# Last feed-forward: two first-half products of six pairs made ahead, reciprocal roots on VectorE, prompt scores as full-height products

## The chip, the cores and the metric

One core of a Trainium2 chip. The metric is device time in microseconds (us) of one launch of the whole kernel, the median over runs. The core has four compute engines, each with its own queue of instructions: TensorE (PE in the profile, with PEld for its weight loads), VectorE (DVE), ScalarE (ACT) and GpSimd (POOL); SyncE (SP) issues the DMAs. Matmuls read SBUF and write PSUM.

## The reference

One step of a two-layer streaming encoder of width 1024 on 640 tokens: 512 of a new prompt and 8 x 16 of running streams. Layer 0 is a convolution module and a feed-forward; layer 1 attends to one shared K/V (16 heads of 64) and has the second feed-forward; a final norm ends it.

```python
def rms_norm(x, g):
    y = x * lax.rsqrt(jnp.mean(x * x, axis=-1, keepdims=True) + EPS)
    return y * g

def swiglu_ffn(h, g, w_in, w_out):
    a, b = jnp.split(rms_norm(h, g) @ w_in, 2, axis=-1)
    return h + (jax.nn.silu(a) * b) @ w_out
...
for l in range(2):
    h = conv_module(h, ...) if l == 0 else h + attention(h) @ w_o
    h = swiglu_ffn(h, norm_ffn[l], w_ffn_in[l], w_ffn_out[l])
return rms_norm(h, norm_final), ...
```

The hidden width of the feed-forward is 2816, that is 22 blocks of 128. Everything is float32.

## The kernel before, in words

Activations lie transposed: 1024 features as 8 tiles of 128 partitions, 640 tokens along the free axis (`h`). A float32 product is made from three products of a reduced type, fp32r: each operand is split into a high part (ScalarE copies it to fp32r) and a low part (VectorE subtracts the high part from the value), and TensorE forms high x high, high x low and low x high (`mm3`, L164 to L166). So each weight tile that comes in by DMA (`raw`) costs one ScalarE and one VectorE pass ahead of its matmuls: L144 and L148 in general, `hilo` (L904, L905) in the last feed-forward.

**Norms.** `colmean` squares the 8 feature tiles, adds `cut` of them up (L187, on GpSimd unless told otherwise) and forms the mean over partitions with tiny matmuls against a column of 1/1024 (L196). `rstd_bc` adds EPS (L217, VectorE), raises to the power -0.5 (L221, GpSimd) and `spread` copies the result to all partitions by a matmul (L208). Twelve places take such a root.

**Attention.** Pairs of heads, with the work of one pair beside the projections of the next. `head_a` makes one prompt head's scores: K lies in 64 of the 128 partitions. KK holds K's high part twice (both halves of the partitions), QQ holds Q's high part in one half and Q's low part in the other, so one product over 128 rows gives two of the three terms (L727); the third, Q high x K low, is a product over 64 rows (L728, KL from L715). The first block of 128 tokens is one plain float32 product over 64 rows (L725). The output projection (L873 adds it to `h`) is split by tokens into 384 and 256 (`SG`).

**The last feed-forward** (from `hf`). Its first matrix product is done as a 2 x 2 block product with seven block products in place of eight: the blocks are feature halves, token halves (320 each, `NH`) and, on the weights' side, the gate and the up columns of one block of 128 (a "pair", 22 of them). X11, X21, ... X22 name the seven operand tiles, kept as high and low parts (`XH`, `XL`), which are made once: `stats` and `xnorm` (L1002) normalise half 0, then half 1, `xsub` forms differences, `xput` (L1012, L1013) splits. `w_seven` makes the weights' side for each pair: four sums of 512 columns (L917 to L923, VectorE) and the splits, in five pieces, into a ring of three 2048-column tiles for each of high and low part; a pair uses two of them. `product` (L936) is one block product, 12 matmuls of 320 columns. `seven` runs the pair: X11, X21, XT2, XT1, XT3, XT4, X22, with ScalarE copies (`keep`, L945) and VectorE additions (`plus`, L951) between, then `gate` (L961) and the split of the hidden tile (L153, L154). The last two products of a pair come after the first ones of the next. After six pairs (four in the last chunk) the output product of that chunk follows (L1075 adds it).

**What sets the order.** A scheduler lists each engine's instructions once, at build time, by priorities (`tc.high_priority(offset=HP)` raises one); on the chip each engine runs its list in order, and waits where an operand is not ready. Tiles of a pool with `bufs=2` are taken in turn: the third user of a name waits for the first to be done.

Of the kernel before, what the change touches and what calls it, by code (L numbers as in the profile page):

```python
# [9 lines left out]
F32R = mybir.dt.float32r  # L10
AF = mybir.ActivationFunctionType
# [3 lines left out]
P = 128  # L15
# [28 lines left out]
HP = 2000  # L44
# [13 lines left out]
SG = ((0, 384), (384, 256))  # L58
# [15 lines left out]
def tile_trunk(ctx, tc, xT, vecs, hist, w_pw1, w_pw2, w_in0, w_out0, w_in1, w_out1,  # L74
# [38 lines left out]
    mhalf = cst.tile([P, 4], F32, name="mhalf", tag="mhalf")  # L113
    nc.gpsimd.memset(mhalf, -0.5)
# [61 lines left out]

    def colmean(st, pieces, n, cut, tag, eng=nc.gpsimd):
        nt = n // P
# [14 lines left out]
        for k, f in enumerate(srcs):  # L193
            s = f()
            for t in range(nt):
                nc.tensor.matmul(st[:, 512 + t * w + k:513 + t * w + k], s[:, t * P:(t + 1) * P],  # L196
                                 onec, start=True, stop=True)
# [8 lines left out]
    def spread(st, r, n):  # L206
        for t in range(n // P):
            nc.tensor.matmul(st[:, t * P:(t + 1) * P], r[:, t:t + 1].to_broadcast([P, P]), ident,  # L208
                             start=True, stop=True)
        return st[:, :n]  # L210

    def rstd_bc(pieces, n, engs=SQ, cut=CUT, r2=None, eng=nc.gpsimd):
        st = w2t()
        nt = n // P
# [6 lines left out]
        nc.gpsimd.tensor_tensor(out=r2[:, :nt], in0=r[:, :nt], in1=mhalf[:, :nt], op=ALU.pow)  # L221
# [478 lines left out]
    def head_a(p, hh):  # L700
# [14 lines left out]
        nc.vector.tensor_tensor(out=KL[r], in0=kt[r, P:], in1=KK[r].bitcast(F32), op=ALU.subtract)  # L715
# [3 lines left out]
        for i in ORD:  # L719
# [4 lines left out]
            if i == 0:  # L724
                nc.tensor.matmul(ps, qt[r, P:2 * P], kt[r, P:2 * P], start=True, stop=True)  # L725
            else:
                nc.tensor.matmul(ps, QQ[:, q], KK[:, 0:n], start=True, stop=False)  # L727
                nc.tensor.matmul(ps, QQ[r, q], KL[r, 0:n], start=False, stop=True)  # L728
# [137 lines left out]
    for g0, n in SG:  # L866
# [15 lines left out]

    mm = fpool("mm2", 6, space=PSUM)
    w2 = fpool("w2b", 1, space=PSUM)
    tp = fpool("tp1", 2)
    wx = fpool("wx", 1)
    xo = fpool("xo", 1)
    XH = xo.tile([P, 7, 4, NH], F32R, name="XH", tag="XH")
    XL = xo.tile([P, 7, 4, NH], F32R, name="XL", tag="XL")
    bcw = xo.tile([P, NT], F32, name="bcw", tag="bcw")  # L890
    xb = ExitStack()
    xt = xb.enter_context(tc.tile_pool(name="xt", bufs=1, reuse_waits="tile"))

    ring = [0]

    def wtile():
        ring[0] += 1
        pool, tag = (wx, "x") if ring[0] % 3 == 0 else (wp, "")
        return (pool.tile([P, 2048], F32R, tag=f"w{tag}hi", name=nm("whi")),
# [282 lines left out]
```

## Time and profile before

| | us |
|---|---|
| median of 3 runs | 1587.42 |
| lowest and highest | 1586.53 and 1593.77 |
| the profiled execution, its own time | 1588.73 |
| its span | 1586.9 |
| TensorE busy | 1500.3 |
| VectorE busy | 1042.2 |
| ScalarE busy | 670.0 |
| GpSimd busy | 401.0 |

The profiled execution had a mean TensorE clock of 0.979 of full speed. In the windows, each row is a stretch of the span (from:to, length), then for each engine busy us and instructions, then the granted clock, the DMA share and GB/s. In the timeline a row is start, duration, engine, line, operation, out<-in, partitions x columns; `64*128` ahead of the shape are the rows and columns of TensorE's array in use. Matmuls are pipelined: the start-to-start step, not the duration, is what one costs.

### The profile page before, as it was taken

What the parts mean: (1) busy time and instruction counts of PE and PEld (TensorE: products, weight loads), DVE (VectorE), ACT (ScalarE), POOL (GpSimd) and SP (SyncE); (2) the same over time, 40 slices, a digit from 0 to 9 for tenths busy, and PEclk for the clock granted to TensorE, in tenths of its full rate; (3) what the DMA queues carried; (4) which work ended last, traced back from release to release, by engine and by line L of the source; (5) the groups of instructions that cost most, each with busy time, mean ns of one, the idle gap of its engine ahead of it and who ended that gap; (6) DMA issues with size and microseconds to landing.
All of it is one profiled execution on the core that took longest, in us unless ns stands there. A gap on an engine that the chain in (4) does not pass through costs nothing.

```text
span 1586.9 us, 26564 instructions
## 1 busy us (share of the span) xinstructions
PE 1500.3 (95%) x10734; PEld 1412.2 (89%) x10734; DVE 1042.2 (66%) x1933; ACT 670.0 (42%) x1228; POOL 401.0 (25%) x368
## 2 busy tenths in 40 slices
PE   5988998999999999999999999998699999999997
PEld 5878898889999999999877887876599999999996
DVE  5895999978535545555665657554785565575565
ACT  4544454535423323234644444443453253253242
POOL 6954577867401000004221112111300000000001
PEclk9999999999999999999999999999799999999998
DMA  7784334444322343335445545451023123122211
GB/s 241 233 235 138 118 119 166 133 160 160 133 74 66 115 146 113 127 113 184 167 151 193 169 165 169 132 183 41 27 80 107 54 80 107 56 90 95 79 55 67
DMA packets 59659, 199.96 MB, mean 126 GB/s; under 512 B 10128, under 2 KB 22672, under 8 KB 46736
## 3 DMA queue, kind: packets, MB, share of 16 engines
q1 hardware_dynamic: 59248, 197.96, 37.7%
q8 instruction: 84, 1.38, 0.4%
q10 hardware_dynamic: 288, 0.31, 0.1%
q14 instruction: 39, 0.32, 0.1%
HBM read 187.02 MB, written 11.22 MB: 125 GB/s over the span
## 4 chain that ended last, share of the span: by engine, by line
PE 73%; DVE 15%; ACT 3%; DMA 3%; POOL 3%; issue 3%; SPq 0%; POOLq 0%; DVEq 0%; ACTq 0%
PE mm L936 17%; PE mm L164 16%; PE mm L166 16%; PE mm L165 16%; DVE w L428 5%; DVE wlo L148 4%; DMA raw<-in_w_pw 1%; PE w L783 1%; PE w L728 1%; DVE xl L154 1%; PE am L814 1%; PE am L768 1%; ACT whi L144 1%; DVE hid L154 1%; PE am L751 1%
## 5 line engine op out<-in xcount | busy, mean ns | idle before, releaser
L165 PE MATMUL mm<-xh,wlo 128*128 128x256 f32 (+1 forms) x1344 | 420.4, 314 | 13.0 <-DVE wlo L148 12.5
L164 PE MATMUL mm<-xh,whi 128*128 128x256 f32 (+1 forms) x1344 | 416.2, 314 | 5.7 <-ACT xh L153 3.6
L166 PE MATMUL mm<-xl,whi 128*128 128x256 f32 (+1 forms) x1344 | 416.6, 313 | 0.7 <-DVE xl L154 0.6
L165 PEld LDWEIGHTS mm<-xh,wlo 128*128 128x128 f32 x1344 | 259.5, 193 | 16.9 <-DVE wlo L148 15.2
L164 PEld LDWEIGHTS mm<-xh,whi 128*128 128x128 f32 x1344 | 257.3, 193 | 11.0 <-ACT xh L153 4.1
L166 PEld LDWEIGHTS mm<-xl,whi 128*128 128x128 f32 x1344 | 257.6, 192 | 2.5 <-DVE xl L154 2.1
L144 ACT ACTIVATE whi<-raw 128x2048 fp32r<-128x2048 f32 (+2 forms) x100 | 170.5, 1708 | 192.2 <-PE mm L166 138.3
L165 PE MATMUL mm<-hid,wlo 128*128 128x320 f32 (+2 forms) x704 | 215.7, 309 | 6.8 <-DVE wlo L148 6.8
L166 PE MATMUL mm<-hid,whi 128*128 128x320 f32 (+2 forms) x704 | 211.8, 308 | 0.2
L148 DVE TENSOR_TENSOR wlo<-raw,whi 128x2048 fp32r<-128x2048 f32 (+5 forms) x100 | 180.7, 1810 | 46.7 <-ACT whi L144 43.9
L164 PE MATMUL mm<-hid,whi 128*128 128x320 f32 (+2 forms) x704 | 210.9, 308 | 0.0
L936 PE MATMUL mm<-XH,whi 128*128 128x320 f32 x616 | 186.1, 314 | 6.2 <-ACT XH L1012 5.1
L936 PE MATMUL mm<-XH,wlo 128*128 128x320 f32 x616 | 191.0, 312 | 0.0
L936 PE MATMUL mm<-XL,whi 128*128 128x320 f32 x616 | 189.8, 311 | 0.0
L148 POOL TENSOR_TENSOR wlo<-raw,whi 128x1536 fp32r<-128x1536 f32 (+3 forms) x50 | 146.5, 2934 | 71.9 <-ACT whi L144 71.7
L165 PEld LDWEIGHTS mm<-hid,wlo 128*128 128x128 f32 x704 | 132.1, 188 | 8.0 <-DVE wlo L148 8.0
L166 PEld LDWEIGHTS mm<-hid,whi 128*128 128x128 f32 x704 | 131.4, 188 | 0.7 <-DVE hid L154 0.6
L164 PEld LDWEIGHTS mm<-hid,whi 128*128 128x128 f32 x704 | 130.7, 188 | 0.4
L221 POOL TENSOR_TENSOR rst<-rst,mhalf 128x2 f32<-128x2 f32 (+1 forms) x9 | 13.6, 1515 | 452.5 <-DVE rst L217 452.5
L936 PEld LDWEIGHTS mm<-XH,whi 128*128 128x128 f32 x616 | 115.6, 190 | 9.0 <-ACT XH L1012 5.8
L936 PEld LDWEIGHTS mm<-XH,wlo 128*128 128x128 f32 x616 | 117.4, 191 | 0.1
L936 PEld LDWEIGHTS mm<-XL,whi 128*128 128x128 f32 x616 | 116.8, 190 | 0.0
(188 smaller groups left out, 2485.3 us busy)
## 6 DMA issues: line engine op xcount, KB each, us to landing
raw<-in_w_in SPq DMA_DIRECT2D x62, 1024.0 KB
raw<-in_w_out SPq DMA_DIRECT2D x36, 768.0 KB
raw<-in_w_pw SPq DMA_DIRECT2D x22, 1024.0 KB
cache<-in_ck SPq DMA_DIRECT2D x32, 512.0 KB
cache<-in_cv SPq DMA_DIRECT2D x32, 512.0 KB
raw<-in_w_kq SPq DMA_DIRECT2D x8, 1024.0 KB
x<-sc SPq DMA_DIRECT2D x16, 368.0 KB
raw<-in_w_out SPq DMA_DIRECT2D x4, 1024.0 KB
```

What stands on the lines that cost most here:

```text
L144: nc.scalar.activation(out=hi[:, a:b], in_=raw[:, a:b], func=AF.Copy)
L148: eng.tensor_tensor(out=lo[:, a:b], in0=raw[:, a:b], in1=hi[:, a:b].bitcast(F32), op=ALU.subtract)
L154: nc.vector.tensor_tensor(out=lo, in0=src, in1=hi.bitcast(F32), op=ALU.subtract)
L164: nc.tensor.matmul(ps, wh, xh, start=(i == 0), stop=False)
L165: nc.tensor.matmul(ps, wl, xh, start=False, stop=False)
L166: nc.tensor.matmul(ps, wh, xl, start=False, stop=(i == last))
L428: nc.vector.scalar_tensor_tensor(out=dst, in0=src, scalar=wj, in1=dst, op0=ALU.mult, op1=ALU.add)
L728: nc.tensor.matmul(ps, QQ[r, q], KL[r, 0:n], start=False, stop=True)
L751: nc.tensor.transpose(tr[:, o:o + P], S[:, SOFF[i] + k * P:SOFF[i] + (k + 1) * P], ident)
L768: nc.tensor.matmul(po[r, k * P:512], VT[:, 1 + k, v0:v0 + DH], PTs[hh][:, POFF[k]:POFF[k] + n], start=(k == 0), stop=(k == 3))
L783: nc.tensor.matmul(st[32 * b:32 * b + 32, 0:512], qv[b], KC[b // 2][:, b % 2, :], start=True, stop=True)
L936: nc.tensor.matmul(pt, w, v[:, x, k, :], start=(first and k == i == 0), stop=(k == 3 and i == 2), skip_group_check=True)
```

## The change

Three things.

1. *The last feed-forward.* The output projection, the norm's statistics and the final norm are split 320/320 instead of 384/256. For the first six pairs, X11 and X21 are made right after the output projection (`early_two`), from a 0.5 MB load of the two weight blocks that they need; t1 and silu(a1) stay in SBUF. Half 1 is normalised meanwhile. These six pairs later need five products each, and one VectorE addition more. The weights' sums are made in place in `raw`, and all four columns of it become one 2048-column high part (ScalarE, one instruction) and one 2048-column low part (VectorE, one instruction); rings of two: `wbig` 2048 columns, `wsmall` 1536 (X11, X21, XT4). The four weight blocks of a pair come in another order from the host.
2. *Roots.* `rsqrt` replaces the power on GpSimd: a bit trick, a scaling and four Newton steps of three operations, all on VectorE, on a few columns.
3. *Scores.* KL is made in both halves of the partitions (two VectorE subtractions of 64 x 512), and every score block is a pair of 128-row fp32r products, KK x QQ and KL x QQ. KL x QQ adds the low x low term. The float32 product and the 64-row products are gone.

```diff
+    def rsqrt(y, v):
+        u = tp.tile([P, 4], F32, tag="rsu", name=nm("rsu"))[:, :y.shape[-1]]
+        nc.vector.tensor_scalar(out=y.bitcast(I32), in0=v.bitcast(I32), scalar1=-0.5,
+                                scalar2=1597463007.0, op0=ALU.mult, op1=ALU.add)
+        nc.vector.tensor_scalar(out=v, in0=v, scalar1=-0.5, scalar2=None, op0=ALU.mult)
+        for _ in range(4):
+            nc.vector.tensor_tensor(out=u, in0=y, in1=y, op=ALU.mult)
+            nc.vector.tensor_tensor(out=u, in0=u, in1=v, op=ALU.mult)
+            nc.vector.scalar_tensor_tensor(out=y, in0=u, scalar=1.5, in1=y, op0=ALU.add,
+                                           op1=ALU.mult)
...
-        nc.gpsimd.tensor_tensor(out=r2[:, :nt], in0=r[:, :nt], in1=mhalf[:, :nt], op=ALU.pow)
+        rsqrt(r2[:, :nt], r[:, :nt])
...
-        nc.vector.tensor_tensor(out=KL[r], in0=kt[r, P:], in1=KK[r].bitcast(F32), op=ALU.subtract)
+        for to in (r, ro):
+            nc.vector.tensor_tensor(out=KL[to], in0=kt[r, P:], in1=KK[r].bitcast(F32),
+                                    op=ALU.subtract)
...
-            if i == 0:
-                nc.tensor.matmul(ps, qt[r, P:2 * P], kt[r, P:2 * P], start=True, stop=True)
-            else:
-                nc.tensor.matmul(ps, QQ[:, q], KK[:, 0:n], start=True, stop=False)
-                nc.tensor.matmul(ps, QQ[r, q], KL[r, 0:n], start=False, stop=True)
+            nc.tensor.matmul(ps, QQ[:, q], KK[:, 0:n], start=True, stop=False)
+            nc.tensor.matmul(ps, QQ[:, q], KL[:, 0:n], start=False, stop=True)
...
+    def w_seven(src, have):
         raw = wp.tile([P, 2048], F32, tag="raw", name=nm("raw"))
         nc.sync.dma_start(raw, src)
+        a11, a12, a22, a21 = (raw[:, 512 * i:512 * i + 512] for i in range(4))
+        vh, vl = wsmall()
+        gh, gl = wbig()
+        sub, add = ALU.subtract, ALU.add
         with tc.high_priority(offset=HP):
+            o = 1024 if have else 0
+            hilo(vh, vl, o, raw[:, o:1536])
+            for out, x, y, op in ((a22, a21, a22, add), (a21, a11, a21, sub),
+                                  (a11, a22, a11, sub), (a12, a12, a11, sub)):
+                nc.vector.tensor_tensor(out=out, in0=x, in1=y, op=op)
+            hilo(gh, gl, 0, raw)
...
+    def early_two(src, jj):
+        ws = w_pre(src)
+        t1, a1 = hid0(jj, F32)
+        pa = mmt()[:, :NH]
         product(pa, ws, X11, True)
+        with tc.high_priority(offset=HP):
+            nc.scalar.activation(out=t1, in_=pa, func=AF.Copy)
+        product(pa, ws, X21, False)
+        with tc.high_priority(offset=HP):
+            nc.scalar.activation(out=a1, in_=pa, func=AF.Silu)
+        return t1, a1
...
+    for jj in range(NPRE):
+        got[jj] = early_two(w_in1[jj], jj)
+        if jj == 1:
+            with tc.high_priority(offset=HP):
+                stats(1)
+                xnorm(x12, 1, 0)
...
```

How each engine's list reads now, at three places. First TensorE, the scores of one prompt head, before (w is the PSUM tile of scores):

```order
5437 L727 MATMUL w_1198_9484<-KK_9486,QQ_9488 128x512
5438 L728 MATMUL w_1198_9484<-KL_9487,QQ_9488 128x512
5439 L727 MATMUL w_1198_9484<-KK_9486,QQ_9488 128x384
5440 L728 MATMUL w_1198_9484<-KL_9487,QQ_9488 128x384
5441 L725 MATMUL w_1198_9484<-kt_9198,qt_9199 128x128
5442 L727 MATMUL w_1199_9485<-KK_9486,QQ_9488 128x256
5443 L728 MATMUL w_1199_9485<-KL_9487,QQ_9488 128x256
```

and the same head now:

```order
5443 L739 MATMUL w_1206_9610<-KK_9612,QQ_9614 128x512
5444 L740 MATMUL w_1206_9610<-KL_9613,QQ_9614 128x512
5445 L739 MATMUL w_1206_9610<-KK_9612,QQ_9614 128x384
5446 L740 MATMUL w_1206_9610<-KL_9613,QQ_9614 128x384
5447 L739 MATMUL w_1206_9610<-KK_9612,QQ_9614 128x128
5448 L740 MATMUL w_1206_9610<-KL_9613,QQ_9614 128x128
5449 L739 MATMUL w_1207_9611<-KK_9612,QQ_9614 128x256
5450 L740 MATMUL w_1207_9611<-KL_9613,QQ_9614 128x256
```

The head keeps its place; one product has become two, and KL reads all 128 rows.

Second TensorE again, between the attention output and the last feed-forward, before (L196 means, L208 spreads the root `rst`, `mm` the PSUM tiles of the first two products of a pair):

```order
6450 L166 MATMUL mm_11470<-olo_11002,whi_11255 128x256
6451 L196 MATMUL w_1517_11511<-onec,acc_11514 128x1 x3
6452 L208 MATMUL w_1517_11511<-ident,rst_1528_11541 128x128 x3
6453 L196 MATMUL w_1531_11569<-onec,acc_11572 128x1 x2
6454 L936 MATMUL mm_11669<-XH,whi_11649 128x320
6455 L936 MATMUL mm_11669<-XH,wlo_11650 128x320
6456 L936 MATMUL mm_11670<-XH,whi_11649 128x320
6457 L936 MATMUL mm_11670<-XH,wlo_11650 128x320
6458 L208 MATMUL w_1531_11569<-ident,rst_1542_11598 128x128 x2
6459 L936 MATMUL mm_11669<-XL,whi_11649 128x320
```

and now, at the end of the early products and the start of the first two full pairs (vhi and vlo are `wsmall`, whi and wlo `wbig`; XH_11650 and XL_11657 are XT1, XH_11649 is XT2):

```order
6616 L956 MATMUL mm_12016<-XH_11648,vlo_12011 128x320
6617 L956 MATMUL mm_12016<-XL_11655,vhi_12010 128x320
6618 L956 MATMUL mm_12061<-XH_11650,whi_12050 128x320
6619 L956 MATMUL mm_12060<-XH_11649,whi_12050 128x320
6620 L956 MATMUL mm_12138<-XH_11650,whi_12108 128x320
6621 L956 MATMUL mm_12118<-XH_11649,whi_12108 128x320
6622 L956 MATMUL mm_12061<-XH_11650,wlo_12051 128x320
6623 L956 MATMUL mm_12061<-XL_11657,whi_12050 128x320
```

Before, four matmuls of the first pair stood ahead of half 1's root, and all others behind it. Now 144 stand there, root and spread of half 1 among them, and behind them come first matmuls of two pairs at once, which read both pairs' whi.

Third VectorE, where one pair's products end and the weights of a later one are made, before (ws is a weight sum, a a PSUM sum):

```order
1289 L951 TENSOR_TENSOR a_1593_11952<-mm_11843,t_1578_11841 128x320
1290 L154 TENSOR_TENSOR hid_11646<-a_1576_11808,hid_11645 128x320
1291 L922 TENSOR_TENSOR ws_12014<-raw_12001 128x512
1292 L923 TENSOR_TENSOR ws_12014<-raw_12001,ws_12009 128x512
1293 L905 TENSOR_TENSOR wlo_12004<-raw_12001,whi_12003 128x1024
1294 L905 TENSOR_TENSOR wlo_12004<-ws_12009,whi_12003 128x1024
```

and now, at the end of the first two full pairs (raw_12199 and raw_12294 are the weights of the third and the fourth, mm_12138 the PSUM tile of the second pair's last product, X22):

```order
1430 L971 TENSOR_TENSOR a_1621_12226<-mm_12118,hid_11783 128x320
1431 L923 TENSOR_TENSOR vlo_12297<-raw_12294,vhi_12296 128x512
1432 L946 TENSOR_TENSOR raw_12199<-raw_12199 128x512
1433 L153 TENSOR_TENSOR hid_12045<-a_1611_12163,hid_12044 128x320
1434 L980 TENSOR_TENSOR a_1621_12226<-a_1621_12226,hid_11784 128x320
1435 L971 TENSOR_TENSOR a_1625_12258<-mm_12138,t_1612_12181 128x320
1436 L946 TENSOR_TENSOR raw_12294<-raw_12294 128x512
1437 L946 TENSOR_TENSOR raw_12199<-raw_12199 128x512
1438 L153 TENSOR_TENSOR hid_12229<-a_1621_12226,hid_12228 128x320
1439 L980 TENSOR_TENSOR a_1625_12258<-b_1614_12197,a_1625_12258 128x320
1440 L946 TENSOR_TENSOR raw_12294<-raw_12294 128x512 x2
1441 L923 TENSOR_TENSOR wlo_12204<-raw_12199,whi_12203 128x2048
```

The sums and low parts of later weights stand among the additions of the running pairs in both; now the fourth sum of the third pair (row 1437) is behind the addition that takes the second pair's last product (row 1435), and the whole of `raw_12199` is ready only after it.

More of the change, by code (lines that the diff above doesn't have):

```diff
@@ L175, in square, with tiles @@
         return q[:, :n]
+    def tiles(n):
+        return [min(t, n - P) for t in range(0, n, P)]
     def colmean(st, pieces, n, cut, tag, eng=nc.gpsimd):
-        nt = n // P
+        nt = len(tiles(n))
         srcs = []
@@ L865, in tile_trunk @@
     wos = [wsplit(w_o[r], 16, P) for r in (2, 3)]
-    for g0, n in SG:
+    for g0, n in ((0, NH), (NH, NH)):
         for m in range(KT):
```

217 lines of the change are left out of this document (114 added, 103 removed).

## The prediction

> **What bounds the kernel now.** First the page's head and the chain that ended last, then the windows by stage, then the waits of TensorE, then single stretches of the timeline.
>
> ```profile
> span 1586.9 us, 26564 instructions
> PE 1500.3 (95%) x10734; PEld 1412.2 (89%) x10734; DVE 1042.2 (66%) x1933; ACT 670.0 (42%) x1228; POOL 401.0 (25%) x368
> PE 73%; DVE 15%; ACT 3%; DMA 3%; POOL 3%; issue 3%; SPq 0%; POOLq 0%; DVEq 0%; ACTq 0%
> ```
>
> TensorE is busy for 95% and carries 73% of the chain. The time can fall in two ways only: fewer TensorE microseconds, or fewer of the 86.6 us in which it does nothing.
>
> ```profile
> core 0: us, PE busy (x) PEld busy (x) DVE busy (x) ACT busy (x) POOL busy (x), PEclk, DMA share, GB/s
> 150.00:400.00 250.00, 226.99 (x1741) 217.20 (x1742) 232.31 (x350) 123.30 (x171) 177.36 (x88) 0.96 0.43 141
> ...
> 765.00:1065.00 300.00, 298.75 (x2459) 245.77 (x2460) 186.76 (x560) 140.22 (x372) 51.34 (x92) 1.00 0.50 167
> 1065.00:1100.00 35.00, 27.32 (x248) 17.40 (x247) 18.27 (x55) 12.83 (x36) 2.03 (x2) 0.90 0.26 90
> ...
> 1125.00:1130.00 5.00, 2.58 (x8) 1.69 (x8) 5.00 (x12) 3.54 (x7) 0.23 (x1) 0.50 0.47 197
> 1130.00:1135.00 5.00, 0.00 (x0) 0.00 (x0) 5.00 (x9) 0.74 (x1) 5.00 (x1) 0.50 0.00 0
> 1135.00:1140.00 5.00, 4.27 (x17) 4.27 (x18) 2.70 (x7) 0.73 (x2) 0.67 (x1) 0.50 0.00 0
> 1140.00:1145.00 5.00, 2.18 (x10) 1.92 (x10) 4.78 (x8) 4.38 (x7) 0.00 (x0) 0.84 0.00 0
> 1145.00:1150.00 5.00, 5.00 (x25) 5.00 (x26) 5.00 (x6) 2.85 (x6) 0.00 (x0) 0.68 0.01 3
> 1150.00:1560.00 410.00, 408.88 (x2756) 406.61 (x2755) 259.01 (x427) 161.62 (x289) 0.00 (x0) 1.00 0.23 78
> ```
>
> The change touches four places. From 150 to 400 VectorE is the tight engine (232 of 250). From 765 to 1065, attention, TensorE is full (298.75 of 300). From 1120 to 1150 lies the hole between the attention output and the last feed-forward: VectorE works through nearly all of it, TensorE hardly. From 1150 to 1560 there is nothing to win: 1.1 us idle in 410, and 2756 matmuls in 408.9 us, about 0.148 each.
>
> ```profile
> PE w L208 <- POOL rst L221: 11.8, 5, 5.9
> ```
>
> TensorE waits five times on GpSimd's root, once for 5.9 us.
>
> **Part 1: the scores.** One head, from TensorE's timeline (start, duration):
>
> ```profile
> 801.36 0.50 PE L727 MATMUL w<-KK,QQ 128*128 128x512 f32 x1
> 801.79 0.50 PE L728 MATMUL w<-KL,QQ 64*128 64x512 f32 x1
> 802.22 0.44 PE L727 MATMUL w<-KK,QQ 128*128 128x384 f32 x1
> 802.60 0.44 PE L728 MATMUL w<-KL,QQ 64*128 64x384 f32 x1
> 802.88 0.38 PE L725 MATMUL w<-kt,qt 64*128 64x128 f32 x2
> 803.19 0.39 PE L727 MATMUL w<-KK,QQ 128*128 128x256 f32 x1
> 803.50 0.38 PE L728 MATMUL w<-KL,QQ 64*128 64x256 f32 x1
> 803.82 0.45 PE L166 MATMUL mm<-xl,whi 128*128 128x384 f32 x1
> ```
>
> Matmuls overlap, so start-to-start counts: 2.46 us a head. For full-height neighbours the steps are these:
>
> ```profile
> 898.68 0.34 PE L164 MATMUL mm<-ohi,whi 128*128 128x384 f32 x1
> 898.85 0.34 PE L165 MATMUL mm<-ohi,wlo 128*128 128x384 f32 x1
> ...
> 901.43 0.28 PE L164 MATMUL mm<-xh,whi 128*128 128x256 f32 x1
> 901.54 0.28 PE L165 MATMUL mm<-xh,wlo 128*128 128x256 f32 x1
> ```
>
> 384 columns step by 0.173, 256 by 0.12. That is 0.053 for 128 columns, which puts 512 at 0.226 and 128 at 0.067 (estimates). The new eight products then take 2 x (0.226 + 0.173 + 0.067 + 0.12) = 1.17 us. [...] The gain is 1.29 us a head.
>
> ```profile
> L715 DVE TENSOR_TENSOR KL<-kt,KK x16: 675/689/735, 755.4 to 1061.9; 64x512 fp32r<-64x512 f32 x16
> ```
>
> The second KL subtraction adds 0.69 us a head to VectorE, 11 us on 187 of 300: room enough while TensorE has other heads' products. The last two heads have no such cover (27.32 of 35 after 1065) and gain nothing: 14 x 1.29 = 18, less 2 x 0.69 for them. **-17 us** (bounds: -20.6 if all sixteen gain; -5 if VectorE becomes the path and 11 us come back).
>
> **Part 2: the hole.** VectorE's steps in it:
>
> ```profile
> 1119.96 1.23 DVE L905 TENSOR_TENSOR wlo<-raw,whi 128x1024 fp32r<-128x1024 f32 x1
> 1121.10 0.15 DVE L217 TENSOR_SCALAR rst<-w 128x3 f32<-128x3 f32 x1
> ...
> 1122.90 0.68 DVE L905 TENSOR_TENSOR wlo<-raw,whi 128x512 fp32r<-128x512 f32 x1
> 1123.51 1.21 DVE L917 TENSOR_TENSOR ws<-raw 128x512 f32<-128x512 f32 x1
> ...
> 1125.24 3.78 DVE L1002 SCALAR_TENSOR_TENSOR xn<-h,vec,bcw 128x320 f32<-128x320 f32 x8
> ...
> 1133.16 0.81 DVE L1013 TENSOR_TENSOR XL<-xn,XH 128x640 fp32r<-128x640 f32 x1
> 1133.90 1.21 DVE L905 TENSOR_TENSOR wlo<-ws,whi 128x1024 fp32r<-128x1024 f32 x1
> ...
> 131.81 0.16 DVE L200 TENSOR_REDUCE mst<-w 128x2 f32<-128x4 f32 x1 [0.42 <-PE w L196]
> 132.00 0.17 DVE L471 COPY mst<-mst 128x2 f32<-128x2 f32 x1
> ...
> L144 ACT ACTIVATE whi<-raw x100: 613/1911/1923, 9.9 to 1052.8; 128x2048 fp32r<-128x2048 f32 x68, 128x1536 fp32r<-128x1536 f32 x24, 128x512 fp32r<-128x512 f32 x8
> ```
>
> Steps: 1024 columns 1.14, 512 0.61, hence 2048 about 2.2; eight norm pieces of 320 3.7 to 3.8; 640 columns 0.74; two tiny operations, the second reading the first, 0.19. A 2048-column high part takes ScalarE 1.91.
>
> Before: the windows from 1125 to 1150 hold 60 matmuls, some ten of them for means and roots. About 50 feed-forward matmuls, worth 7 us, in the 30.5 us since the attention output ended (1119.5): 23 lost. After, with zero at 1119.5: VectorE does half 0 (eight norm pieces 3.7, four XL 3.0, from 0.6), then the fifteen Newton operations of half 1 and their sum, 3.0: 10.3. Then, in program order, four 1024 low parts 4.6, eight norm pieces 3.7, eight differences 5.9, ten XL 7.4, two 512 low parts 1.2 and eight weight sums 4.9, up to 38. Only then can ScalarE form the two 2048-column high parts of the first two full pairs (to 39.8 and 41.7), and VectorE the low part of the first (42). TensorE's next four matmuls take the high parts of both pairs, the fifth a low part. The 144 early matmuls (six pairs, two products of twelve; 21.3 us) are long done by then, at about 30 with their own stalls. So at 42 TensorE has lost 20.7, and about 2 more to the lower clock: in the windows 1135 to 1140 it was granted 0.50 after the idle stretch. **0**: the early products fill the old hole, and a new one opens behind them, because VectorE's queue sets both. (Bounds: -12, if the sums could go ahead of the XL; +6.)
>
> **Part 3: inside the six pairs.** The early pairs run in twos, ten products a group, and one big weight tile lies ahead. At both later group starts, VectorE's fourth sum for the next pair stands behind the add that takes the last X22 product. From that product's end: add 0.49 (below), two sums 1.2, high part 1.9, low part 2.2, signals about 0.5: 6.3 us in which TensorE has two matmuls, and about 1.5 us of clock behind it.
>
> ```profile
> L961 DVE TENSOR_TENSOR a<-mm,a x22: 479/490/492, 1163.4 to 1546.6; 128x320 f32<-128x320 f32 x22
> ```
>
> 2 x 7.8 = **+15.5** (bounds +4 and +20). Later chunks: one low part behind such an add, about 1 us, three times: +3. Before, pieces of 512 and 1024 let a product begin on its own piece; now all 2048 must be there. The feed-forward as a whole: 0 + 15.5 + 3 = **+18.5**.
>
> **Part 4: roots elsewhere.**
>
> ```profile
> 1568.48 0.16 DVE L217 TENSOR_SCALAR rst<-w 128x3 f32<-128x3 f32 x1 [0.23 <-PE w L196]
> 1568.78 0.85 POOL L221 TENSOR_TENSOR rst<-rst,mhalf 128x3 f32<-128x3 f32 x1 [433.11 <-DVE rst L217]
> ```
>
> From L217 to the end of the power is 1.15 us; fifteen dependent steps of 0.19 make 2.85: +1.7 wherever nothing covers it, at the start and at the end. [...] The trace's dependent pair says 0.19, and I go by it. Start +1.7; end +2.3 (the last half is 320 wide, not 256: eight pieces of 0.47 for 320 columns, some 0.06 more each by the step of 0.61 for 512); conv stage, where VectorE is tight and three or four roots lie, +3 (0 to 9, all of their instructions at 0.15 being the upper bound).
>
> **The sum.** -17 + 18.5 + 1.7 + 2.3 + 3 = +8.5 on an execution of 1588.73 (span 1586.9). The median stands 1.3 lower, at 1587.4: **1596 us**. About 0.5% (8 us) is what a measurement of this kernel can tell from no change.
>
> **Rivals.**
> *The hole closes and no new one opens* (faster). If the sums and high parts run while the early products do, the full pairs start at 30, not 42, and group starts cost 2 us. The point that decides is whether VectorE finishes the eighth weight sum before about 28 on my scale. For it: TensorE's idle time in the old hole was a wait on GpSimd (5.9), which goes. Against: VectorE was full there already. Feed-forward 0 - 14 + 4 = -10, all told -17 - 10 + 7 = -20: about 1567; with the roots free too, 1562.
> *VectorE takes back the scores* (slower). Its second KL subtraction stands ahead of QQ in every head, and each score waits for both. If VectorE's 62% are more in the stretches where a head starts, 11 to 12 of the 17 us return: 1596 + 11 = 1607. It decides where TensorE's idle time from 765 to 1065 exceeds 10 us. For it: in the changed order TensorE comes to each head sooner. Against: only 1.25 of 300 idle now.
> *The products keep their step* (the change does not do what it says): 0.43 belongs to the 512 columns and not to the change of rows. Then only the f32 product's part goes, gain 5: 1608. Against it stands the 256-column pair, 0.31 a product beside 0.12 elsewhere.
>
> **How the numbers follow.** The forecast's case has 0.49, own range 1586 to 1606: 0.26 of it lies within 8 us of no change, 0.23 beyond. The hole that closes 0.33, 0.30 of it faster; VectorE takes back 0.11, the kept step 0.03, both slower; 0.04 for things not thought of, half of it faster. Faster 0.32, same 0.29, slower 0.39. The range runs from the closed hole with all sixteen heads gaining, 1567 - 3 = 1564, to the slower rivals, 1609.
>
> **What would show it.** Right: in attention the scores step by 0.23 and 0.17, and the wait on GpSimd's root is gone; TensorE idle for some 10 us after 144 early products, waiting on ScalarE's whi, and again twice for about 6, waiting on VectorE's wlo; Newton chains of about 2.9 us. Wrong: fewer than 5 us idle between the early products and the first XT1, no gap at the group starts, over 10 us idle in attention, or tiny operations at 0.07.

## The result: 52 us slower, and the profile after

The changed kernel takes 1639.3 us (median of 4 runs, 1638.5 to 1639.7) beside 1587.6 for the kernel before: a ratio of 1.032, interval 1.029 to 1.034. The forecast was 1596, in a range of 1564 to 1609; the direction was right, the size was not. The head of the changed kernel's page:

```profile
span 1637.9 us, 26669 instructions
PE 1501.2 (92%) x10766; PEld 1424.5 (87%) x10766; DVE 1094.1 (67%) x2078; ACT 659.4 (40%) x1154; POOL 374.9 (23%) x346
```

TensorE's busy time hardly moved (1500.3 before); it stands still for 137 us in place of 87. By landmarks of the two timelines (the first score of attention and four later points), the 51.0 us between the two spans divide so:

| stretch | before | after | difference |
|---|---|---|---|
| start to the first score (start, convolution, first feed-forward, K/V) | 763.8 | 793.5 | +29.7 |
| to the first addition of the last output projection (attention) | 330.7 | 318.6 | -12.1 |
| to the end of the sixth pair's products (504 matmuls) | 127.4 | 145.6 | +18.2 |
| to the last output addition (16 pairs, three chunks) | 353.8 | 364.3 | +10.5 |
| to the end | 11.2 | 15.9 | +4.7 |

The windows that answer to those of before, in the convolution stage and around the last feed-forward:

```profile
core 0: us, PE busy (x) PEld busy (x) DVE busy (x) ACT busy (x) POOL busy (x), PEclk, DMA share, GB/s
150.00:400.00 250.00, 211.18 (x1595) 202.10 (x1594) 226.87 (x374) 114.92 (x160) 165.53 (x86) 0.92 0.39 127
...
1150.00:1200.00 50.00, 37.74 (x227) 35.12 (x227) 36.88 (x52) 23.04 (x34) 0.00 (x0) 0.89 0.30 105
1200.00:1250.00 50.00, 36.98 (x214) 35.66 (x213) 34.69 (x55) 14.20 (x18) 0.00 (x0) 0.83 0.23 74
```

From 150 to 400 TensorE is busy for 211 us where it was 227. From 1150 to 1250 it idles for 25 of 100 us; the kernel before was full from 1150 on (408.88 of 410).

And TensorE's waits:

```profile
PE w L210 <- DVE rst L222: 22.9, 4, 11.3
...
PE mm L956 <- ACT whi L922: 19.1, 4, 8.1
...
PE mm L956 <- DVE wlo L923: 6.6, 5, 1.5
```

The wait on GpSimd's root has gone, as forecast. A longer one on VectorE's root has its place: four waits, one of 11.3 us. That one, on VectorE's timeline:

```profile
158.28 0.16 DVE L230 TENSOR_SCALAR rst<-w 128x2 f32<-128x2 f32 x1 [4.69 <-PE w L198]
158.47 0.17 DVE L216 TENSOR_SCALAR rst<-rst 128x2 int32<-128x2 int32 x1
158.55 0.55 DVE L399 SCALAR_TENSOR_TENSOR gp<-t,t 128x384 f32<-128x384 f32 x1
...
159.74 0.15 DVE L221 TENSOR_TENSOR rsu<-rsu,rst 128x2 f32<-128x2 f32 x1
159.87 0.62 DVE L441 SCALAR_TENSOR_TENSOR w<-gp,dwv,w 128x384 f32<-128x384 f32 x1
160.40 2.05 DVE L222 SCALAR_TENSOR_TENSOR rst<-rsu,rst 128x2 f32<-128x2 f32 x1
162.37 1.21 DVE L147 TENSOR_TENSOR wlo<-raw,whi 128x1024 fp32r<-128x1024 f32 x1
...
169.29 0.15 DVE L222 SCALAR_TENSOR_TENSOR rst<-rsu,rst 128x2 f32<-128x2 f32 x1
```

Two things are to be seen. Between the steps of the chain stand rows of other work: a convolution tap of 0.62 us, a low part of 1.21. And one step of two elements took 2.05 us. What GpSimd did meanwhile:

```profile
160.09 2.34 POOL L147 TENSOR_TENSOR wlo<-raw,whi 128x1024 fp32r<-128x1024 f32 x1 [2.51 <-ACT whi L143]
```

The step ends at 162.45, GpSimd's subtraction at 162.43. From the sum (158.28) to the last step's end (169.44) are 11.2 us, where in the kernel before the power ended 1.2 us after the sum. In the new list the scheduler has put 14 other rows between sum and last step, and VectorE does them in that order.

The held step is not alone. In the chain of the first root five steps took 0.50 to 0.94 us each, and in that of the fourth root the scaling took 3.24; each of them ended within 0.03 us of the end of a GpSimd instruction:

```profile
214.06 3.48 POOL L147 TENSOR_TENSOR wlo<-raw,whi 128x1536 fp32r<-128x1536 f32 x1 [4.59 <-ACT whi L143]
214.33 3.24 DVE L218 TENSOR_SCALAR rst<-rst 128x2 f32<-128x2 f32 x1
```

These three chains (the first, third and fourth of the twelve roots; below they are the exposed ones) take 31.5 us from sum to last step together, and hold some 7.7 us of such lengthening beyond 0.17 us a step. So two things make a chain long: the rows between its steps, and single steps that end only with GpSimd's instruction.

The second hole and a group start, from TensorE's timeline:

```profile
1174.11 0.31 PE L956 MATMUL mm<-XL,vhi 128*128 128x320 f32 x1
1182.47 0.90 PE L956 MATMUL mm<-XH,whi 128*128 128x320 f32 x2 [8.06 <-ACT whi L922]
1184.27 0.63 PE L956 MATMUL mm<-XH,whi 128*128 128x320 f32 x1 [0.90 <-ACT whi L922]
...
1208.67 0.90 PE L956 MATMUL mm<-XH,whi 128*128 128x320 f32 x2 [5.08 <-ACT whi L922]
1211.01 0.63 PE L956 MATMUL mm<-XH,wlo 128*128 128x320 f32 x1 [1.43 <-DVE wlo L923]
```

and what VectorE did at that group start:

```profile
1204.93 0.48 DVE L971 TENSOR_TENSOR a<-mm,t 128x320 f32<-128x320 f32 x1
1205.34 1.28 DVE L946 TENSOR_TENSOR raw<-raw 128x512 f32<-128x512 f32 x2
...
1208.67 2.28 DVE L923 TENSOR_TENSOR wlo<-raw,whi 128x2048 fp32r<-128x2048 f32 x1
```

The attention output ended at 1140.8. The early products ended 33.6 us later (forecast about 30). The full pairs' first matmul came after 41.7 us, where the forecast had its high part at 39.8, and the first one on a low part (1184.97) after 44.2, where it had 42: both some 2 us late. The two group starts stand still for 5.1 + 1.4 and 5.0 + 1.5 us, where the forecast had 6.3: the addition after the last X22, two sums, the high part, the low part.

### The profile page after: what moved, and what is told of

It reads as the page before. It is cut to its first block, busy times and chain, and to the rows that moved or that the text cites. A ratio compares the mean times of both kernels' runs of the same rounds, so it can differ in the third digit from the quotient of the medians.

```text
span 1637.9 us, 26669 instructions
## 1 busy us (share of the span) xinstructions
PE 1501.2 (92%) x10766; PEld 1424.5 (87%) x10766; DVE 1094.1 (67%) x2078; ACT 659.4 (40%) x1154; POOL 374.9 (23%) x346
## 3 DMA queue, kind: packets, MB, share of 16 engines
q8 instruction: 84, 1.38, 0.3%
## 4 chain that ended last, share of the span: by engine, by line
PE 74%; DVE 17%; DMA 3%; issue 2%; ACT 2%; POOL 0%; SPq 0%; DVEq 0%; ACTq 0%; POOLq 0%
PE mm L164 17%; PE mm L163 17%; PE mm L165 16%; PE mm L956 16%; DVE w L441 4%; DVE wlo L147 4%; PE am L780 1%; DVE xl L153 1%; PE w L795 1%; DMA x<-sc 1%; PE am L826 1%; PE am L763 1%; ACT whi L143 1%; DMA cache<-in_ck 1%; PE mm L473 1%
## 5 line engine op out<-in xcount | busy, mean ns | idle before, releaser
L164 PE MATMUL mm<-xh,wlo 128*128 128x256 f32 (+1 forms) x1344 | 419.8, 314 | 19.4 <-DVE wlo L147 19.3
L143 ACT ACTIVATE whi<-raw 128x2048 fp32r<-128x2048 f32 (+2 forms) x100 | 170.3, 1708 | 189.2 <-PE mm L165 150.0
L164 PE MATMUL mm<-hid,wlo 128*128 128x320 f32 (+2 forms) x560 | 172.6, 310 | 4.9 <-DVE wlo L147 4.7
L165 PE MATMUL mm<-hid,whi 128*128 128x320 f32 (+2 forms) x560 | 169.8, 309 | 0.0
L163 PE MATMUL mm<-hid,whi 128*128 128x320 f32 (+2 forms) x560 | 168.5, 309 | 1.1 <-DVE h L307 0.7
L956 PE MATMUL mm<-XH,whi 128*128 128x320 f32 x352 | 111.3, 322 | 19.1 <-ACT whi L922 19.1
L956 PE MATMUL mm<-XH,wlo 128*128 128x320 f32 x352 | 113.2, 322 | 6.6 <-DVE wlo L923 6.6
L956 PE MATMUL mm<-XL,whi 128*128 128x320 f32 x352 | 111.2, 320 | 0.0
L164 PEld LDWEIGHTS mm<-hid,wlo 128*128 128x128 f32 x560 | 105.8, 189 | 6.0 <-DVE wlo L147 5.5
L441 DVE SCALAR_TENSOR_TENSOR w<-gp,dwv,w 128x384 f32<-128x384 f32 x180 | 105.3, 613 | 1.0
L163 PEld LDWEIGHTS mm<-hid,whi 128*128 128x128 f32 x560 | 104.5, 189 | 1.6 <-DVE h L307 0.9
L165 PEld LDWEIGHTS mm<-hid,whi 128*128 128x128 f32 x560 | 105.2, 189 | 0.0
L922 ACT ACTIVATE whi<-raw 128x2048 fp32r<-128x2048 f32 (+2 forms) x38 | 55.4, 1481 | 84.8 <-PE mm L165 50.3
L956 PEld LDWEIGHTS mm<-XH,whi 128*128 128x128 f32 x352 | 69.1, 199 | 20.2 <-ACT whi L922 20.2
```

What stands on the lines that cost most here:

```text
L143: nc.scalar.activation(out=hi[:, a:b], in_=raw[:, a:b], func=AF.Copy)
L163: nc.tensor.matmul(ps, wh, xh, start=(i == 0), stop=False)
L164: nc.tensor.matmul(ps, wl, xh, start=False, stop=False)
L165: nc.tensor.matmul(ps, wh, xl, start=False, stop=(i == last))
L441: nc.vector.scalar_tensor_tensor(out=dst, in0=src, scalar=wj, in1=dst, op0=ALU.mult, op1=ALU.add)
L922: nc.scalar.activation(out=hi[:, a:b], in_=src, func=AF.Copy)
```

## Experiments

Each of the three parts was put alone into the kernel before, then taken apart. All times are medians beside runs of the kernel before on the same chip (1586.4 to 1589.0).

**The roots alone.**

```diff
-        nc.gpsimd.tensor_tensor(out=r2[:, :nt], in0=r[:, :nt], in1=mhalf[:, :nt], op=ALU.pow)
+        rsqrt(r2[:, :nt], r[:, :nt])
```

> The kernel before with only the roots changed: four Newton steps on VectorE in place of the power on GpSimd. Theory A (the root's latency in VectorE's queue): three roots of the start and the conv stage end 7, 10 and 12 us later after their sums than before, each with other VectorE operations between its steps, so the scores start some 29 us later and the kernel takes 1617 to 1622 us. Theory B (the roots are cheap and the conv stage lost its time to something else in the change): 1588 to 1594 us.

Measured: 1629.5 us (1624.7 to 1630.0), ratio 1.026 (1.024 to 1.028). The first score comes 27.5 us later (791.3), near theory A's 29; the hole ahead of the last feed-forward grows by 6 us and the end by 4.6, more than it had, so the time lies above its 1617 to 1622. Theory B is out. (The profiled execution is the fastest of the four, 1624.7; the stretches are read from it, and the other 5 us of the median are not in them.) TensorE's waits up to the first score, in the kernel before:

```profile
PE mm L165 <- DVE wlo L148: 19.3, 17, 3.6
...
PE mm L164 <- ACT xh L153: 3.6, 2, 2.6
PE w L208 <- POOL rst L221: 2.4, 2, 1.3
```

and with the roots alone:

```profile
PE mm L164 <- DVE wlo L147: 24.0, 17, 4.1
PE w L207 <- DVE rst L219: 20.1, 3, 11.3
...
PE mm L163 <- ACT xh L152: 6.3, 3, 3.4
```

Waiting for roots went from 2.4 to 20.1 us: 17.7 of the 27.5. Another 4.7 are additional waits on low parts of weights and 2.7 on high parts of activations (`xh`). That these come from the moved order of VectorE's rows fits the run with unawaited chains below, which has them too, but is not shown by itself.

**One Newton step in place of four.** The roots are then only good to about 0.2%.

```diff
-        for _ in range(4):
+        for _ in range(1):
```

> As the roots alone, but with one Newton step in place of four (the roots are then only good to about 0.2%). Theory A: the chain is 6 operations long instead of 15, each with the same neighbours between, so about 6/15 of the 29 us stay: 1597 to 1602 us. Theory C (the delay comes from the moved order of the conv stage, not from the length of the chain): the same time as with four steps, within 4 us.

Measured: 1615.9 us, ratio 1.017 (1.015 to 1.019). Neither: the first score is still 24.5 us late. The chains did get short (3 to 7 us from sum to spread at the three exposed roots in place of 8 to 13), but the second of these roots' sums came 13 us late (161.49 against 148.80). Part of this is order: a low part of 2.29 us now stands ahead of the layer norm's mean on VectorE, which it followed before. The rest is not traced.

**No step at all**, the bit trick and the scaling alone; the roots are good to some per cent.

```diff
-        for _ in range(4):
+        for _ in range(0):
```

> The roots alone, with no Newton step: the bit trick and the scaling, so the roots are only good to some per cent. Theory A (length of the chain): three operations in place of fifteen, the scores start less than 6 us later than before, the kernel under 1600 us. Theory C (the moved order of the conv stage): the scores still start over 15 us later, the kernel takes 1603 us or more.

Measured: 1594.2 us, ratio 1.0046 (1.0031 to 1.0061). In the profiled execution (1601.2, the longest of its runs) the first score is 8.3 us late, a little more than theory A allowed, far under theory C. Roots of three operations on VectorE (sum, bit trick, scaling) still gain nothing over GpSimd's power.

**The chain beside the old roots**, with nobody waiting for it.

```diff
         nc.gpsimd.tensor_tensor(out=r2[:, :nt], in0=r[:, :nt], in1=mhalf[:, :nt], op=ALU.pow)
+        nc.vector.tensor_scalar(out=d2[:, :nt], in0=r[:, :nt], scalar1=1.0, scalar2=None,
+                                op0=ALU.mult)
+        rsqrt(d[:, :nt], d2[:, :nt])
```

> The kernel before, its roots still from GpSimd, with the whole Newton chain (and one copy) made beside them on VectorE for nothing: nobody waits for its result. Theory A (the waiters wait for the chain's end): no change but for the load, 1587 to 1594 us. Theory C (the additional rows shift VectorE's list and what others wait for): the scores start over 10 us later, 1600 us or more.

Measured: 1600.1 us, ratio 1.008 (1.006 to 1.011); the first score is 12.3 us late. So the rows alone, unawaited, cost almost half of what the roots cost up to there, and theory C's bounds hold. Up to the first score TensorE waited 25.5 us on low parts of weights (19.3 before) and 8.4 on high parts of activations (3.6 before); its waits on roots did not grow (2.1).

**The three exposed roots left on GpSimd**, nine others as chains.

```diff
-        rsqrt(r2[:, :nt], r[:, :nt])
+        site[0] += 1
+        if site[0] not in (1, 3, 4):
+            rsqrt(r2[:, :nt], r[:, :nt])
+        else:
+            nc.gpsimd.tensor_tensor(out=r2[:, :nt], in0=r[:, :nt], in1=mhalf[:, :nt], op=ALU.pow)
```

> The roots alone, but the three exposed ones of the start and the conv stage (the first norm's root of the sample group, the layer norm's and the feed-forward norm's of the same group) stay on GpSimd; nine others are Newton chains. Theory A (those three chains' lengths, 6.9, 10.0 and 10.2 us more between sum and spread, are the conv stage's loss): the scores start within 5 us of before, the kernel takes 1594 to 1603 us, what is left being the last feed-forward's norm and the end. Theory C (any added rows on VectorE reorder the conv stage): the scores start 10 us later or more, 1606 us or more.

Measured: 1613.6 us, ratio 1.016 (1.015 to 1.018); the first score 14.9 us late. Theory A fails as put: 12.6 us come back, not 22 or more, and theory C's bounds hold. Another root, which nobody waited for before, now shows (one wait of 3.0 on a chain).

**Is the conv stage simply full?** Two kernels leave out 15 of the 31 taps of the convolution where VectorE makes it, one with the old roots, one with the chains.

```diff
-        for j in range(W):
+        for j in range(16):
```

> The kernel before with 15 of the 31 taps of the depthwise convolution left out where VectorE makes it (not where TensorE does), so that VectorE has room in the conv stage. It is the base for the next run: some 40 to 60 us faster than before, since each tap that goes is about 0.6 us and the stage is bound by VectorE.

Measured: 1585.7 us, ratio 0.998 (0.997 to 0.9998). No 40 us: nearly nothing. Its windows:

```profile
0.00:150.00 150.00, 122.73 (x962) 112.21 (x962) 90.26 (x139) 71.18 (x118) 100.86 (x122) 0.97 0.71 212
150.00:400.00 250.00, 226.92 (x1742) 218.13 (x1742) 199.25 (x266) 126.43 (x174) 177.81 (x89) 0.96 0.44 147
```

VectorE has 51.5 us less to do up to 400 (108.7 and 232.3 before), TensorE the same 350. What the prediction read as VectorE being the tight engine was in large part filling, which others did not wait for.

> The same with the Newton roots. Theory E (the roots cost so much because VectorE's list is tight in the conv stage: what is put in, or put elsewhere, delays all behind it): the scores start less than 14 us later than in the light kernel, about half of the 27.5 us with all taps. Theory F (chains and list cost what they cost, tight or not): 20 to 30 us later, as with all taps.

Measured: 1627.4 us, ratio 1.024 (1.022 to 1.026); the first score 26.5 us later than in the light kernel. Theory E falls, theory F holds. TensorE's waits up to there:

```profile
PE mm L164 <- DVE wlo L147: 22.5, 17, 3.6
PE w L207 <- DVE rst L219: 20.7, 3, 11.3
```

The root is waited for as long as with all taps: the scheduler put rows that are left between the steps, 14 of them in the chain that is waited for longest, as many as with all taps.

**The chain kept together**, fourteen rows on VectorE with nothing between, each waiting for the one before by a semaphore.

```diff
+        with tc.tile_critical():
+            then(nc.vector.tensor_scalar(out=y.bitcast(I32), in0=v.bitcast(I32), scalar1=-0.5,
+                                         scalar2=1597463007.0, op0=ALU.mult, op1=ALU.add))
...
```

> The roots alone, with each Newton chain of fourteen rows kept together on VectorE: no other row stands between two of its steps (each waits for the one before it by a semaphore of its own). Theory A2 (the chains are long because other rows stand between their steps, most of 0.62 us, one up to 2): from the sum to the spread some 3 to 4 us at the three exposed roots in place of 8 to 13, the scores start 6 to 13 us later than before in place of 27.5, the kernel takes 1600 to 1611 us. Theory C2 (the list around the chains is what costs): the chains are short, but the scores start over 20 us later, 1618 us or more.

Measured: 1660.2 us, ratio 1.047 (1.044 to 1.049). A miss, and not a test of what it was made for. The steps do run at 0.195 us (twelve of them from 171.03 to 173.34), but the block as a whole begins later than its data, and 5 to 12 us pass at each root from the sum to the spread; the first score comes 54 us late. At the first root VectorE sat idle for 8.05 us between the sum (14.43) and the block's first row (22.62). Rows of the second exposed root, with a wait of 0.74 at the block's start and a first step that again ended with a GpSimd subtraction (168.43 to 170.77):

```profile
168.87 1.92 DVE L223 TENSOR_SCALAR rst<-rst 128x2 int32<-128x2 int32 x1 [0.74 <-DMA raw<-in_w_pw]
171.03 0.16 DVE L227 TENSOR_TENSOR rsu<-rst 128x2 f32<-128x2 f32 x1
171.22 0.16 DVE L228 TENSOR_TENSOR rsu<-rsu,rst 128x2 f32<-128x2 f32 x1
```

Keeping a chain together by such a block brought waits of its own, so neither theory is decided by it.

**The scores alone** (the third piece of the change's diff, in the kernel before).

> The kernel before with only the scores changed. Theory A (TensorE's time in the scores falls, most of it reaches the end): 12 to 17 us faster than before, 1570 to 1576 us. Theory B (VectorE's second KL subtraction gives it back): 1583 us or more.

Measured: 1575.0 us, ratio 0.992 (0.991 to 0.994). Theory A, at the lower end. One head:

```profile
800.21 0.50 PE L726 MATMUL w<-KK,QQ 128*128 128x512 f32 x1
800.54 0.39 PE L727 MATMUL w<-KL,QQ 128*128 128x512 f32 x1
800.77 0.34 PE L726 MATMUL w<-KK,QQ 128*128 128x384 f32 x1
800.95 0.35 PE L727 MATMUL w<-KL,QQ 128*128 128x384 f32 x1
801.14 0.22 PE L726 MATMUL w<-KK,QQ 128*128 128x128 f32 x1
801.20 0.27 PE L727 MATMUL w<-KL,QQ 128*128 128x128 f32 x1
801.31 0.33 PE L726 MATMUL w<-KK,QQ 128*128 128x256 f32 x1
801.48 0.28 PE L727 MATMUL w<-KL,QQ 128*128 128x256 f32 x1
801.59 0.34 PE L166 MATMUL mm<-xl,whi 128*128 128x384 f32 x1
```

1.38 us where it was 2.46; 512 columns step by 0.23 behind a 512, 384 by 0.18, as worked out. The first product of this head, which follows one on 64 x 32 tiles, still steps by 0.33. That is half of the 0.21 that the estimate of 1.17 had too little; the other half lies in the smaller products, most of it in one 256 that steps by 0.17 and one 128 that steps by 0.11. So 1.08 a head, not 1.29. The heads that follow a full-height product gain no more: 1.28 where it was 2.35. From the first score to the first addition of the output projection the gain is 13.6 us: 12.4 up to the fifteenth head and 1.2 from there on, where the forecast had 18 and a loss of 1.4.

**The scores and one root.** On top of the scores, only the root that took GpSimd 5.9 us becomes a chain.

```diff
-            bc, _ = rstd_bc([h[:, k, a:a + n] for k in range(KT)], n)
+            bc, _ = rstd_bc([h[:, k, a:a + n] for k in range(KT)], n, newt=g0 > 0)
```

> The scores alone, with one more edit: the root of half 1 ahead of the last feed-forward, which took GpSimd 5.9 us, is a Newton chain on VectorE, all others stay. If the chain runs as it did with the roots alone (1.3 us of wait in place of 5.9): 3 to 5 us faster than the scores alone, 1570 to 1572 us. If VectorE's other work stands between its steps: no gain, 1575 us or more.

Measured: 1577.2 us, ratio 0.993 (0.992 to 0.995): no gain. TensorE's wait for that root fell to 3.1 us, but from the sum to the spread passed 10.0 us (6.2 before), with 12 other rows of VectorE between, and TensorE then waited 6.5 for the operand tiles, where VectorE was the later one.

**The feed-forward alone** (power on GpSimd, scores as before).

> The changed kernel with the power on GpSimd and the scores as before: only the last feed-forward is changed. Theory A (its own gaps, 8 and 1.4 us before the full pairs and 5 and 1.4 us at two group starts): 18 to 26 us slower than before, 1605 to 1613 us, with the gaps in the trace. Theory B (the gaps there come from the Newton chain): 1590 us or less.

Measured: 1620.9 us, ratio 1.020 (1.019 to 1.022), 34 us slower. Theory A's gaps are there without any Newton chain, so theory B is out; the loss is larger than expected, since the later chunks lose 10.5 us, which theory A did not have. TensorE's waits in its last feed-forward:

```profile
PE mm L948 <- ACT whi L914: 17.1, 4, 5.8
PE mm L948 <- DVE wlo L915: 6.6, 5, 1.5
```

**The same with the big tile in two pieces.** XT1 and XT3 need only the first two sums.

```diff
-                nc.vector.tensor_tensor(out=out, in0=x, in1=y, op=op)
-            hilo(gh, gl, 0, raw)
+                nc.vector.tensor_tensor(out=out, in0=x, in1=y, op=op)
+                if i % 2:
+                    hilo(gh, gl, (1024, 0)[i // 2], raw[:, (1024, 0)[i // 2]:(2048, 1024)[i // 2]])
```

> The last feed-forward alone, with the big weight tile split into two pieces of 1024 columns, the first of them (XT1 and XT3) after the first two sums. Theory A (a group start waits for the fourth sum and for the whole tile): the two gaps of 5.0 and 1.4 us at the group starts fall to under 3 us together each, and the first one by some 2 us, so 1606 to 1613 us in place of 1621. Theory D (VectorE has too much to do in the six pairs, whatever the order): the gaps move but stay, 1617 us or more.

Measured: 1600.1 us, ratio 1.009 (1.006 to 1.011): 21 us of the 34 come back, more than expected, since the chunks' three stalls went as well (353.3 us there, 353.8 before, 364.3 in the change).

```profile
PE mm L949 <- DVE wlo L915: 5.1, 3, 2.9
PE mm L949 <- ACT whi L914: 4.6, 4, 2.6
```

So the whole tile behind the fourth sum was the cause of those stalls. The gaps at the two group starts fell from 6.5 us each to 4.3 and 1.7 (under 3 expected), the one ahead of the full pairs from 7.0 to 3.8. The stretch from the end of the output projection to the 504th product stays 10 us longer than before.

**The eight differences moved to GpSimd.**

```diff
-            nc.vector.tensor_tensor(out=out[i], in0=a[i], in1=b[i], op=ALU.subtract)
+            nc.gpsimd.tensor_tensor(out=out[i], in0=a[i], in1=b[i], op=ALU.subtract)
```

> The split feed-forward with the eight differences of the operand tiles (5.9 us of VectorE) on GpSimd, which is idle there. Theory A (VectorE's queue between the early products and the first full pairs sets the second hole): 3 to 7 us faster than with the split alone, 1593 to 1597 us. Rival (GpSimd's own durations, some three times VectorE's, become the path, or both engines get in each other's way): 1600 us or more.

Measured: 1607.5 us, ratio 1.013 (1.011 to 1.014), 7 us slower than the split alone: the rival. A difference took GpSimd 1.7 to 2.5 us (VectorE 0.8), and VectorE's low parts beside them took up to 2.2 us in place of 0.8. Taking 5.9 us off VectorE does not help if GpSimd does it; so this run does not say whether VectorE's queue alone sets the second hole.

**Scores and split feed-forward.**

> The changed kernel with the power on GpSimd and the split weight tile. If the parts add up, it is 12 us faster than the split feed-forward alone: 1594 to 1601 us, so still slower than the scores alone (1575). If the scores' gain needs the old output projection, less than 6 us faster.

Measured: 1590.7 us, ratio 1.002 (1.001 to 1.003). The parts add up in the main (9 us below the split alone, where 12 would be all of it); the expected 1594 to 1601 was reckoned from a slower split than was measured. Up to the first addition of the output projection the new scores gain 9 us beside the new feed-forward (318.4 against 327.6) and 13.6 without it. The sum is still behind the scores alone. The best version of all is the kernel before with the scores: 1575.0.

## Why the prediction was wrong

*Part 1, the scores: right, a size off.* -12.1 against -17; alone, the scores gave -12.0. Of the -12.1 some 2.3 belong to the output projection in 320/320, since in the feed-forward alone, with the old scores, that stretch is 2.3 us shorter, too. The sum's 1.29 us a head is 1.08, because neither the first product of a head nor the smaller ones fall as far as estimated, and TensorE waits somewhat more (3.8 of 291 us idle in the scores alone, 2.1 of 305 before). The rival that VectorE takes the gain back did not come, nor the one that the products keep their step.

*Parts 2 and 3, hole and group starts: right.* The full pairs begin 41.7 us after the output projection (39.8 forecast), the group starts stand still for 6.5 (6.3). From the end of the output projection, the zero of the forecast, to the 504th product the loss is 14.9 (116.9 against 102.0); the forecast had 0 + 15.5. The 18.2 of the table hold 3.3 more because the projection itself, whose first addition comes sooner, spreads over 28.7 us in place of 25.4. In the forecast's 6.3 the 0.5 for signals was the author's estimate, as were the 1.5 of clock behind it; no run shows the first by itself. Behind the second group start the clock was granted at 0.50 and 0.72 (1235 to 1240, 1240 to 1245), and 320 columns stepped by 0.27 in place of 0.15 sixteen times, about 2 us. The rival of a hole that closes is out. The split tile showed the mechanism at the group starts. That VectorE's queue sets the second hole is read from the trace, where VectorE pauses for only 0.7 us between 1154.1 and 1182.4; no run isolates it.

*Part 3, later chunks: right mechanism, a third of the size.* +10.5 against +3. The windows at the first and the third of the three stalls:

```profile
1327.00:1332.00 5.00, 3.07 (x18) 2.54 (x17) 3.98 (x4) 3.14 (x5) 0.00 (x0) 0.96 0.05 7
1332.00:1337.00 5.00, 5.00 (x27) 5.00 (x26) 4.34 (x8) 1.37 (x3) 0.00 (x0) 0.70 0.52 206
...
1567.00:1572.00 5.00, 3.07 (x20) 2.55 (x18) 3.98 (x4) 3.39 (x5) 0.00 (x0) 1.00 0.00 0
1572.00:1577.00 5.00, 5.00 (x37) 5.00 (x36) 4.57 (x8) 1.24 (x3) 0.00 (x0) 1.00 0.63 210
```

At each stall TensorE waits 0.7 us on a high part of `wsmall` and 1.2 on a low part of `wbig`. At the first, 45 matmuls go through in ten us where 68 go into a full stretch, a loss of 3.3: the waits and the lower clock (0.70) behind them. At the second it is much the same (0.76). At the third the clock stayed at 1.00 after the same waits, and 57 went through, a loss of 1.6. Together that is some 8 of the 10.5 us. The working had 1 us, only the low part and no clock.

*Part 4, the roots: the step that failed, the cost of a root on VectorE.* "Fifteen dependent steps of 0.19 make 2.85", hence +1.7 at the start and +3 in the conv stage, with 9 as the upper bound. Measured up to the first score: +29.7 in the change, +27.5 alone; and +4.7 against +2.3 at the end, where the roots alone cost 4.6 and the feed-forward alone 0.8. The 0.19 a step is right where nothing else is in the list, as at the very end (1626.60 to 1629.19 for fourteen steps). It is wrong where VectorE has other rows, because the scheduler puts them between the steps, and where GpSimd works beside, because there some single steps (2.05 and 3.24 us the longest) ended only with its instruction. At the three exposed roots, 8 to 13 us passed between sum and spread. Roots that are free and tiny operations at 0.07, which the prediction also weighs, no run shows: alone a step took 0.15 to 0.17, dependent ones started 0.195 apart, and roots of three operations on VectorE still came to 1594.2. The order of the changed kernel lay open when the sum was made, and VectorE's list in the conv stage has a row between most steps of the second and third of these chains; the prediction read the chain from two rows of a quiet place instead. The light kernels show a second error in the same part: the stage was called tight because VectorE was busy for 232 of 250 us, and with 51.5 us less of its work the kernel was only 0.2% faster. Without the roots (+7) the forecast came to +1.5, so that its direction was right owes much to terms that were far too small.

*What is settled and what is not.* That the roots cause the 27.5 us is shown by putting them in alone. That 17.7 of them are waits on a root is read from the trace, and so are the two things that make those chains long. How the rest divides, between chains at other roots and the moved list, is not settled: the additions do not add up (12.3 for rows that nobody awaits, 12.6 back for three roots left out, 24.5 with chains a third as long), and each version has another list from the scheduler. The run that was to hold the list still brought waits of its own. Alone, the three parts make +42, +34 and -12, together 64 against 52. By the spans of the profiled executions it is +36.1, +32.7 and -14.0, together 54.8 against 51.0; much of the gap of 12 is thus that these executions differ from the medians, that of the roots alone most (4.7 us under its median). Of the stretches, the hole loses 9.4 us less in the full change than the parts together (no root is waited for there any more, where the roots alone wait 12.2 us), attention gains 3.8 less, and the later chunks lose 2.2 more. Why attention and chunks differ is not traced.

## What to carry to other kernels

A chain of tiny dependent operations costs as many queue positions as it has steps: on an engine whose list is filled by a scheduler, count the rows that stand between the steps in the new order, not the steps alone (fourteen steps took 2.6 us with none between, and 11.0 with other rows between and one step held), and look for what GpSimd does at the same time. A share of busy time near one does not make an engine the bound of its stage (VectorE was busy for 232 of 250 us, and 51.5 us less of its work gained 0.2%); leave some of its work out and see. And a weight tile that is made in one piece made the first product wait for the last sum (two pieces brought back 21 of 34 us): split it where the consumers split.

## What the runs showed of the hardware

- A VectorE step on two elements took 2.05 us and ended with GpSimd's subtraction beside it (162.45 and 162.43), where it takes 0.15 alone. This step reads two tiles. A step that reads one was held as well: 3.24 us from 214.33, to 217.57, with GpSimd's subtraction ending at 217.54. Why such a step is held, no run here shows.
- Dependent VectorE steps of two or three elements start 0.195 us apart, at the end of the changed kernel (1626.88 to 1629.03) and in the block kept together (171.03 to 173.18) alike.
- Two waits close together, 0.7 and 1.2 us, were followed by a lower granted clock in the next window at two of three places (0.70 and 0.76; 320 columns then step by 0.27 us in place of 0.15) and by 1.00 at the third. The loss was 3.3 us for 1.9 us of waits at the first place and 1.6 at the third: at the first the waits cost more than themselves, at the third they did not.
- In the kernel before, a 512-column product stepped by 0.33 to 0.43 us where the next product changed between 128 and 64 rows; with the scores alone it stepped by 0.23 where both had 128. There the first product of a head stepped by 0.33 behind one on 64 x 32 tiles (800.21); behind 128 x 128 products with `ident` it stepped by 0.31 (805.52), so the tiles are not the only reason.
